# Two merge-gate tiles projected inside the attention stage of a hybrid mixer kernel

## The chip, the cores and the metric

The kernel runs on one core of one Trainium2 chip. The metric is the device time of one execution in microseconds (us). A measurement of it is the median of several executions.

## The reference, cut to what matters

Two layers work on 1024 latent tokens and 256 context tokens of width 1024. In the last layer the context gives keys and values alone, so most projections run over 1280 tokens in layer 0 and over 1024 in layer 1. Everything is float32.

```
z = split_cols(h @ w_in)                     # 54 column tiles of 128 and a short one
y_mla  = dense_attention(...)                # 4 heads, 1280 keys
y_diff = two dense attentions, p1 - lam * p2 # 4 heads, 1280 keys
y_swa  = windowed attention with sinks       # 4 heads, 3 blocks of 128 keys + 256 context keys
y_pool = windowed means, a small matmul
gates  = silu(z.gates)                       # 1024 columns = 8 tiles
mgate  = sigmoid(z.merge)                    # 4096 columns = 32 tiles, 8 for each branch
m = sum_r mgate[r] * ((ys[r] * gates[r]) @ w_br[r])
x = x + gate * rms_norm(m @ w_out)
lam = exp(sum(lam_q1*lam_k1)) - exp(sum(lam_q2*lam_k2)) + lam_init
```

## The kernel before, in words

Activations lie with channels on the partitions. Each float32 matmul is done as three products of rounded halves (`mm3`, L74). A projection tile is 128 columns of `w_in`: for each chunk of tokens (512, 512 and, in layer 0 or for keys and values, 256) it takes 8 steps over the 1024 input channels, and a step is one `mm3`. So a tile is 72 matmuls over 1280 tokens (48 of 512 columns, 24 of 256) and 48 matmuls over 1024 tokens. Its weights come by one transfer of 512 KB (`wraw`), are split into `wh` on ACT and `wl` on POOL, and lie in two buffers; `Dense.step` (L321) asks for the weights of the next tile when it begins one.

A layer has these stages: the latent projections; the other projections, first those that differential attention needs; attention (L1193: units of differential, then MLA, then windowed attention, which is the local branch); the merge (L1400); the output projection.

What is not needed for the first attention units waits in a list of filler tiles (L762 to L772): gates 0 to 6, the tile of windowed values, that of windowed keys, two of windowed queries, two pooling tiles with their small work behind each, gate 7. Attention calls `dense.fill(us)` (L341) after each score block and each step of the probability-times-value products; `fill` adds to an account and issues steps of the list while the account is positive. A step of 512 tokens costs 0.648 in the account's own units, one of 256 half of that; a tile over 1280 tokens costs 12.96, one over 1024 costs 10.37. The amounts stand in `FILL` (L1562): `"pre"` is spent before the first unit; the entries 2, 1 and 3 are the amount for a unit of differential, MLA and windowed attention, shared over its calls (9, 7 and 5 in a full unit; a unit of the context block has fewer). When the list is empty, `fill` does nothing.

Each engine runs its instructions in a fixed order, that of a planner which takes the program's order as priority and moves an instruction forward where it judges it ready first. All transfers are issued by SP's one queue, in such an order too.

In the merge, for each of 32 tiles (branch r, tile d), the gate tile is projected (`st.body`, L1423), its PSUM leaves through a sigmoid on ACT into `sg` (three buffers of 512 tokens, one of 256), and the branch's product of the tile before (`branch_mm`, L1363) is issued after the first 8 steps. DVE multiplies that product with `sg`, POOL adds it to the sum `m`. `st.load` at the head of a tile asks for the weights of the next.

The constants of attention (four rows for lambda, the sinks, the mask) are loaded after the first unit's keys and queries (`const_loads`, L957) and ahead of the "pre" filling.

Of the kernel before, what the change touches and what calls it, by code (L numbers as in the profile page):

```python
# [32 lines left out]
def kernel(ctx: ExitStack, tc: tile.TileContext, A: dict, out: bass.AP):  # L33
# [73 lines left out]
    xmid = dram.tile([KT, 128, SEQ], F, name="xmid")  # L107
    yd = [dram.tile([4, 128, T], F, name=f"yd{r}") for r in range(4)]
    zgd = dram.tile([8, 128, T], F, name="zgd")
    mq = dram.tile([2, 4, 96, T], R, name="mq")  # L110
    mk = dram.tile([2, 4, 64, T], R, name="mk")
    mkr = dram.tile([2, 32, T], R, name="mkr")
# [388 lines left out]
    def layer(l, es_prev):  # L501
# [15 lines left out]
        def lat_tile(i, dt):  # L517
            return (p1 if i > 2 else p1b).tile([128, T], dt, name=f"n{i}", tag=f"n{i}")
# [172 lines left out]
        def gates(j):  # L691
            def ev(ps, c0, n):
                z = f32("zc", n)
                act(z, ps)
                dma(zgd[j, :, c0:c0 + n], z)
            dense.tile(st, W_G + j, qch, ev)

        def pooled():
            LP = 8 + SEQ + 8 + CTX + 8
            H_, L_ = slice(64, 128), slice(0, 64)  # L700
            wph = p2.tile([128, 2, 128], R, name="wph", bufs=1)
            wpl = p2.tile([128, 2, 128], R, name="wpl", bufs=1)
            spc = p2.tile([128, 2], F, name="spc", bufs=1)
            keep = {}

            def pos(c0):
                return c0 + 8 if c0 < SEQ else c0 + 16

            def weights():
                wpr = f32("zc", 256).rearrange("p (a b) -> p a b", a=2)  # L710
                nc.gpsimd.memset(wpr, 0.0)
                for g in range(4):
                    o = 64 * (g % 2)
                    dma(wpr[o:o + 64, g // 2, o:o + 64], A["w_pool"][l, g])
                split(wpr, wph, wpl)
                dma(spc, A["s_pool"][l].rearrange("(j p) -> p j", p=128))

            for j in range(2):
                def ev(ps, c0, n, j=j):
                    if c0 == 0:  # L720
                        vals.drain()
                        if j == 0:
                            weights()
                        keep[j] = p2.tile([128, LP], F, name="up", tag="zt1", bufs=1)
                        nc.gpsimd.memset(keep[j], 0.0)
                    act(keep[j][:, pos(c0):pos(c0) + n], ps)
                dense.tile(st, W_POOL + j, qch, ev)

                def rest(j=j):
                    for c0, n in qch:  # L730
                        up = keep[j][:, pos(c0) - 8:pos(c0) + n + 8]
                        w = n + 16
                        a = f32("t1", w)
                        b = f32("t2", w)
                        tt(a[:, 1:w], up[:, 0:w - 1], up[:, 1:w], ALU.add)
                        if j == 0:
                            tt(b[H_, 8:8 + n], a[H_, 7:7 + n], a[H_, 9:9 + n], ALU.add)
                        else:
                            tt(b[:, 2:w - 1], a[:, 1:w - 2], a[:, 3:w], ALU.add)
                            tt(a[:, 4:w - 3], b[:, 2:w - 5], b[:, 6:w - 1], ALU.add)  # L740
                            tt(b[H_, 8:8 + n], a[H_, 4:4 + n], a[H_, 12:12 + n], ALU.add)
                        yield 0.3 * n / 512
                        nc.vector.tensor_copy(out=b[L_, 8:8 + n], in_=a[L_, 8:8 + n])
                        rc = f32("tab", n)
                        dma(rc, A["rcnt"][j, :, c0:c0 + n])
                        t1 = f32("tab", n)
                        tt(t1, b[:, 8:8 + n], rc, ALU.mult)
                        tt(t1, t1, up[:, 8:8 + n], ALU.subtract)
                        hl_ = {}
                        spl(t1, lambda h: hl_.__setitem__(0, h), lambda h: hl_.__setitem__(1, h))  # L750
                        ps = dense_ps(n)
                        mm3(ps, lambda k: wph[:, j], lambda k: wpl[:, j], lambda k: hl_[0], lambda k: hl_[1], [0], 1)
                        yv = f32("zc", n)
                        act(yv, ps, scale=spc[:, j:j + 1])
                        dma(yd[0][j, :, c0:c0 + n], yv)
                        yield 0.4 * n / 512
                dense.add(f"pool{j}", None, rest)
# [5 lines left out]
        values(W_DV + 1, dvd, 2)  # L763
        roped(W_DK, dkd, ALL, 1.0, 8, 16, ("C32", "S32"))
        roped(W_DQ, dqd.rearrange("m a d n -> a m d n"), qch, 32 ** -0.5, 8, 16, ("C32", "S32"))
        for j in range(7):
            gates(j)
        values(W_SV, svd, 0)
        keys_swa()
        roped(W_SQ, sqd, qch, 64 ** -0.5, 4, 32, ("C64", "S64"))  # L770
        pooled()
        gates(7)  # L772

        p1b = pool(f"mlb{l}", 1, es_m)

# [5 lines left out]
        def wsplit(name, r0, rows, cols):  # L781
# [4 lines left out]
            split(raw, h, lo)  # L786
            return h, lo

        gkv = gcol("g_ckv", 0, 128)
        gq0 = gcol("g_cq", 0, 128)  # L790
        gq1 = gcol("g_cq", 128, 64)
# [97 lines left out]
        def up_all():  # L889
            nonlocal kvh, kvl, q0h, q1h, q0l, q1l  # L890
            for us in key_rope():
                yield us
            kvh, kvl, q0h, q0l = (lat_tile(i, R) for i in (0, 3, 1, 4))
            q1h, q1l = (lat_tile(i, R)[0:64] for i in (2, 5))
            todo = [(0, c) for c in ALL] + [(1, c) for c in qch]
# [51 lines left out]
        c1 = pool(f"ac{l}", 1, es_a)  # L947

        smask = c1.tile([128, 768], F, name="smask")
        ls = c1.tile([128, 2], F, name="ls")  # L950
        nlam = c1.tile([128, 1], F, name="nlam")
        sink = c1.tile([128, 4], F, name="sink")
        nsink = c1.tile([128, 4], F, name="nsink")
        lam = kp.tile([128, T], F, name="P", tag="P", bufs=5)[:, 0:128].rearrange("p (a c) -> p a c", a=4)
        lt = kp.tile([128, T], F, name="P", tag="P", bufs=5)[:, 0:64].rearrange("p (a c) -> p a c", a=2)

        def const_loads():  # L957
            for i, n in enumerate(("lam_q1", "lam_k1", "lam_q2", "lam_k2")):
                dma(lam[:, i], A[n][l:l + 1, :].broadcast_to([128, 32]))
            dma(sink, A["sink"][l:l + 1, :].broadcast_to([128, 4]))  # L960
            dma(smask, A["smask"])

        def const_values():
            lv = lam.rearrange("p (a b) c -> p a b c", b=2)
            tt(lt, lv[:, :, 0], lv[:, :, 1], ALU.mult)
            nc.vector.tensor_reduce(out=ls, in_=lt, axis=AX.X, op=ALU.add)
            act(ls, ls, AF.Exp)
            tt(nlam, ls[:, 1:2], ls[:, 0:1], ALU.subtract)
            ts(nlam, nlam, -lam_init, op0=ALU.add)
            ts(nsink, sink, -1.0)  # L970
# [246 lines left out]

        todo = []
        prefetch(0)
        const_loads()  # L1220
        dense.fill(FILL[l]["pre"])
        const_values()
        last.clear()
        for i, (key, keys, load, run) in enumerate(units):
            mains, after = run(kvs[key], qts.pop(i))
            us, turns = FILL[l][key[0]], TURNS[key[0]]
            f = us / (len(mains) + sum(turns)) if i else 1.6
            for a, main in enumerate(mains):
                main()
                if a == 0:  # L1230
                    prefetch(i + 1)
                dense.fill(f)
                n = turns[a]
                while todo and (todo[0][0] < i - 1 or a and n):
                    todo.pop(0)[1]()
                    dense.fill(f)
                    n -= 1
            todo += [(i, g) for g in after()]
            nxt = units[i + 1][0][0] if i + 1 < len(units) else None
            if nxt != key[0] and key[0] != 2:  # L1240
                close_row(key[0])
# [3 lines left out]
        while pend:  # L1245
            dense.fill(1.0)
            pend.pop(0)()
        dense.until(W_G + 7)
        es_a.close()
        es_p.close()  # L1250

# [147 lines left out]

        for q, (r, d) in enumerate(order):  # L1400
            i = W_M + r * 8 + d
            if q + 1 < len(order):
                st.load((l, i + 1))
            else:
                st.load((l, W_O), use=0)
            braw = tp.tile([128, 2, 128], F, name="braw", tag="braw", bufs=1)
            dma(braw, A["w_br"][l, r, d])
            bh = tp.tile([128, 2, 128], R, name="bh", tag="bh")
# [1 line left out]
            split(braw, bh, bl)  # L1410
            sg = {}

            def ev(ps, c0, n, sg=sg):
                if n == 512:
                    sg[c0] = tp.tile([128, 512], F, name="sg", tag="sg", bufs=3)
                else:
                    sg[c0] = tp.tile([128, 256], F, name="sgc", tag="sgc", bufs=1)
                act(sg[c0], ps, AF.Sigmoid)
            if r < 3 and d == 4:
                prep.add(gated_y(r + 1, 0), 0.0)  # L1420
            if r and d == 0:
                prep.add(gated_y(r, 1), 0.0)
            body = st.body((l, i), qch, ev)  # L1423
            some(body, KT)
            if prev:
                if prev[1] == 0:
# [104 lines left out]
        for q, (ci, d) in enumerate(steps):  # L1531
# [27 lines left out]
        es_l.close()  # L1559
        return es_t  # L1560

    FILL = ({1: 4.1, 2: 4.9, 3: 0.8, "n": 1.5, "uk": 1.2, "uq": 1.5, "uv": 2.0, "pre": 10.0},  # L1562
            {1: 4.3, 2: 4.9, 3: 0.8, "n": 2.5, "uk": 1.2, "uq": 1.5, "uv": 2.0, "pre": 8.0})
    TURNS = {1: (3, 2), 2: (2, 1, 1, 1), 3: (1, 2)}
    GY = (3.0, 1.5, 1.3, 0.5)
    WMB = 6
# [111 lines left out]
```

## Time and profile before

| what | value |
|---|---|
| median of 3 runs | 2753.53 us (2751.33 to 2753.72) |
| profiled execution | 2753.32 us, of it 2751.5 us from the first to the last instruction |
| TensorE's granted clock over the span | 0.978 of full |
| busy: PE, weight load, DVE, ACT, POOL | 95%, 80%, 55%, 43%, 29% |
| layer 0: attention, merge begins | 250 us, about 811 us |
| layer 1: attention, merge begins | 1696 us, about 2197 us |

The page of the profile gives busy time by engine and by slice of the span. The view of instructions by line and shape gives counts and mean durations; the view of stretches gives busy time between two moments; the view in order of time gives single instructions. PE is the matmul engine. A matmul's row is as long as the matmul takes from its start to its last result, and the next begins before that, so PE's busy time overlaps itself and is no measure of how many columns go through.

### The profile page before, as it was taken

To read this page: it belongs to the slowest core of one execution; us is meant where nothing else is said; L and a number is where in the kernel's file an instruction comes from. 1 tells how busy PE (TensorE), PEld (TensorE's weight loads), DVE (VectorE), ACT (ScalarE), POOL (GpSimd) and SP (SyncE) were. 2 spreads that over 40 slices of the span, in tenths; PEclk is the share of its full clock that TensorE was granted. 3 is DMA by queue.
4 is the path that set the end of the run, shared out by engine and by line. 5 is a ranking of instruction groups with operands and counts; after the bars stand their busy time and mean duration, and the time that the engine had idled before them with its cause. 6 is when DMAs were issued, how large, how long until landed. Compare 5 with 4: busy or idle time off the path is not lost.

```text
span 2751.5 us, 38436 instructions
## 1 busy us (share of the span) xinstructions
PE 2616.2 (95%) x14194; PEld 2199.9 (80%) x14194; DVE 1519.6 (55%) x2638; ACT 1186.6 (43%) x2178; POOL 802.3 (29%) x492
## 2 busy tenths in 40 slices
PE   7997999999989989999999997999999999999998
PEld 5776888888878878888878776888877788888878
DVE  7545788766754894332148554888666732233133
ACT  4433677655662212222245443777555722222231
POOL 4223333110002224443324313443110022444324
PEclk9998999999999999999999998999999999999999
DMA  6366333533334652221135266333432243222123
GB/s 237 98 194 202 121 96 92 148 117 96 95 113 141 196 164 77 77 74 61 35 107 193 90 203 210 116 106 113 132 104 91 79 128 103 79 86 87 48 77 100
DMA packets 209069, 322.27 MB, mean 117 GB/s; under 512 B 26740, under 2 KB 123634, under 8 KB 208882
## 3 DMA queue, kind: packets, MB, share of 16 engines
q1 hardware_dynamic: 208882, 319.83, 37.2%
q8 instruction: 111, 1.82, 0.3%
q14 instruction: 76, 0.62, 0.1%
HBM read 239.07 MB, written 77.86 MB: 115 GB/s over the span
## 4 chain that ended last, share of the span: by engine, by line
PE 61%; DVE 9%; issue 4%; DMA 4%; ACT 2%; POOL 1%; SPq 1%; POOLq 0%; DVEq 0%; ACTq 0%
PE pd L76 12%; PE pd L77 12%; PE pd L78 12%; PE acc L1021 5%; PE pt L1005 4%; PE pt L76 2%; PE pt L77 2%; PE pt L78 2%; DVE mjunk L150 2%; PE pss L1116 1%; PE pss L1075 1%; PE pss L1076 1%; PE pss L1077 1%; PE pd L1546 1%; PE pss L1174 1%
## 5 line engine op out<-in xcount | busy, mean ns | idle before, releaser
L76 PE MATMUL pd<-h,wh 128*128 128x512 f32 (+2 forms) x2288 | 857.8, 375 | 20.0 <-ACT zt L50 9.5
L78 PE MATMUL pd<-h,wl 128*128 128x512 f32 (+2 forms) x2288 | 845.4, 370 | 0.0
L77 PE MATMUL pd<-h,wh 128*128 128x512 f32 (+2 forms) x2288 | 844.6, 369 | 0.0
L53 POOL TENSOR_TENSOR wl<-wraw,wh 128x1024 fp32r<-128x1024 f32 x106 | 260.7, 2459 | 988.9 <-ACT wh L50 915.3
L76 PEld LDWEIGHTS pd<-h,wh 128*128 128x128 f32 (+1 forms) x2288 | 436.4, 191 | 83.4 <-ACT sg L50 10.2
L78 PEld LDWEIGHTS pd<-h,wl 128*128 128x128 f32 (+1 forms) x2288 | 435.2, 190 | 67.6 <-issue 1.5
L77 PEld LDWEIGHTS pd<-h,wh 128*128 128x128 f32 (+1 forms) x2288 | 436.6, 191 | 59.0 <-DVE h L56 0.8
L53 DVE TENSOR_TENSOR tl<-pt,th 128x512 fp32r<-128x512 f32 (+1 forms) x420 | 276.3, 671 | 135.0 <-ACT th L50 131.4
L977 DVE CUSTOM_DVE_ANT_0 P<-pss,zero 128x1280 f32<-128x1280 f32 (+1 forms) x216 | 295.9, 1370 | 97.4 <-PE pss L1116 46.1
L50 ACT ACTIVATE th<-pt 128x512 fp32r<-128x512 f32 (+1 forms) x420 | 239.7, 582 | 159.7 <-PE pt L1005 153.1
L53 DVE TENSOR_TENSOR sg<-sg,pt 128x512 f32<-128x512 f32 x96 | 65.6, 687 | 391.0 <-PE pt L78 390.5
L1005 PE MATMUL pt<-kc,P 128*128 128x128 f32 x1632 | 256.2, 276 | 4.8 <-DVE P L56 1.2
L1021 PE MATMUL acc<-th,vt 128*128 128x256 f32 x816 | 244.9, 312 | 3.4 <-ACT ot L50 1.5
L1021 PE MATMUL acc<-tl,vt 128*128 128x256 f32 x816 | 222.0, 293 | 9.5 <-DVE tl L53 8.9
L50 ACT ACTIVATE wh<-wraw 128x1024 fp32r<-128x1024 f32 x124 | 130.8, 1055 | 221.6 <-PE pd L77 169.1
L50 ACT ACTIVATE P<-P,m 128x1280 f32<-128x1280 f32 (+1 forms) x144 | 182.7, 1269 | 75.5 <-DVE m L977 74.7
L50 ACT ACTIVATE sg<-pd 128x512 f32<-128x512 f32 x128 | 75.7, 591 | 311.7 <-PE pd L78 304.4
L1005 PEld LDWEIGHTS pt<-kc,P 128*128 128x128 f32 x1632 | 191.8, 142 | 20.2 <-DVE tl L53 6.3
L53 POOL TENSOR_TENSOR m<-m,sg 128x512 f32<-128x512 f32 x96 | 131.3, 1373 | 209.9 <-DVE sg L53 208.7
L1021 PEld LDWEIGHTS acc<-th,vt 128*128 128x128 f32 x816 | 155.7, 191 | 37.6 <-ACT th L50 20.5
L1021 PEld LDWEIGHTS acc<-tl,vt 128*128 128x128 f32 x816 | 156.1, 191 | 29.5 <-DVE tl L53 20.3
L50 ACT ACTIVATE P<-P,negm 128x1280 f32<-128x1280 f32 (+3 forms) x144 | 146.5, 1017 | 75.2 <-DVE negm L977 74.6
(291 smaller groups left out, 3918.2 us busy)
## 6 DMA issues: line engine op xcount, KB each, us to landing
wraw<-in_w_in_dram SPq DMA_DIRECT2D x108, 512.0 KB, 3.6
wmt<-in_w_modt_dram SPq DMA_DIRECT2D x64, 256.0 KB, 3.0
wraw<-in_w_out_dram SPq DMA_DIRECT2D x32, 512.0 KB, 3.2
yd<-ot SPq DMA_DIRECT2D x108, 128.0 KB, 1.8
kt<-dkd SPq DMA_DIRECT2D x64, 160.0 KB, 3.2
qt<-dqd SPq DMA_DIRECT2D x72, 128.0 KB, 2.8
ya<-yd SPq DMA_DIRECT2D x36, 256.0 KB, 3.0
yb<-yd SPq DMA_DIRECT2D x36, 256.0 KB, 3.0
```

The costliest lines, as they stand in the source:

```text
L50: return nc.scalar.activation(out=o, in_=i, func=func, **kw)
L53: return (e or nc.vector).tensor_tensor(out=o, in0=a, in1=b, op=op)
L76: nc.tensor.matmul(ps, wh(k), xh(k), start=k == 0, stop=False)
L77: nc.tensor.matmul(ps, wh(k), xl(k), start=False, stop=False)
L78: nc.tensor.matmul(ps, wl(k), xh(k), start=False, stop=k == n - 1)
L150: nc.vector.tensor_tensor_reduce(out=jk, in0=a, in1=b, scale=1.0, scalar=start, op0=ALU.mult, op1=ALU.add, accum_out=o)
L977: nc.vector.tensor_tensor_reduce(out=o, in0=i, in1=zero.to_broadcast([128, nk]) if mask is None else mask, scale=-1.0, scalar=1e30 if h is ...
L1005: t = nc.tensor.transpose(pt[:, 2 * j + i, :], Ps[i][:, (g + j) * 128:(g + j + 1) * 128], ident)
L1021: nc.tensor.matmul(acc, vt[:, kts[g + j], :], x[:, j, :], start=g + j == 0 and a == 0, stop=g + j == nk - 1 and a == 1)
L1075: nc.tensor.matmul(o, qt[0:96, 0, qs], kh[0:96, ks], start=True, stop=False)
L1076: nc.tensor.matmul(o, qt[0:96, 0, qs], kl[0:96, ks], start=False, stop=False)
L1077: nc.tensor.matmul(o, qt[0:96, 1, qs], kh[0:96, ks], start=False, stop=True)
```

## The change

Gate 7 joins gates 0 to 6 at the head of the filler list. At its end come two merge-gate tiles, `W_M + 26` and `W_M + 29` (branch 3, tiles 2 and 5). They leave PSUM through a copy on ACT and go to memory (`zmd`). In the merge these two tiles load no weights and issue no projection: each chunk is read back from `zmd` into `sg` and takes its sigmoid there. The loads of the tiles around them skip them. The four lambda rows and the sinks are loaded earlier, before the latent up-projections, and the lambda sums are formed there; the mask is loaded in the third attention unit. `FILL` has new amounts.

```diff
-        for j in range(7):
+        for j in range(8):
             gates(j)
...
         pooled()
-        gates(7)
+        early = [W_M + 26, W_M + 29]
+        for e, i in enumerate(early):
+            merge_gate(e, i)
...
+        def merge_gate(e, i):
+            def ev(ps, c0, n):
+                z = f32("zc", n)
+                act(z, ps)
+                dma(zmd[e, :, c0:c0 + n], z)
+            dense.tile(st, i, qch, ev)
...
+        lam = p1.tile([128, 4, 32], F, name="lam")
+        for i, n in enumerate(("lam_q1", "lam_k1", "lam_q2", "lam_k2")):
+            dma(lam[:, i], A[n][l:l + 1, :].broadcast_to([128, 32]))
+        dma(sink, A["sink"][l:l + 1, :].broadcast_to([128, 4]))
...
         prefetch(0)
-        const_loads()
         dense.fill(FILL[l]["pre"])
...
                 if a == 0:
                     prefetch(i + 1)
+                    if i == 2:
+                        dma(smask, A["smask"])
...
-        dense.until(W_G + 7)
+        dense.until(early[-1])
...
-            if q + 1 < len(order):
-                st.load((l, i + 1))
-            else:
+            if q + 1 == len(order):
                 st.load((l, W_O), use=0)
+            elif i not in early:
+                st.load((l, i + 2 if i + 1 in early else i + 1))
...
+            def reload(e, sg_tile=sg_tile):
+                for c0, n in qch:
+                    s = sg_tile(c0, n)
+                    dma(s, zmd[e, :, c0:c0 + n])
+                    for k in range(KT - 1):
+                        yield 0.0
+                    act(s, s, AF.Sigmoid)
+                    yield 0.0
...
-            body = st.body((l, i), qch, ev)
+            body = reload(early.index(i)) if i in early else st.body((l, i), qch, ev)
...
-    FILL = ({1: 4.1, 2: 4.9, 3: 0.8, "n": 1.5, "uk": 1.2, "uq": 1.5, "uv": 2.0, "pre": 10.0},
-            {1: 4.3, 2: 4.9, 3: 0.8, "n": 2.5, "uk": 1.2, "uq": 1.5, "uv": 2.0, "pre": 8.0})
+    FILL = ({1: 3.95, 2: 6.8, 3: 1.45, "n": 1.5, "uk": 1.2, "uq": 1.5, "uv": 2.0, "pre": 15.0},
+            {1: 3.9, 2: 5.9, 3: 1.45, "n": 2.5, "uk": 1.2, "uq": 1.5, "uv": 2.0, "pre": 13.0})
```

## Rows read from the trace of the kernel before

**Rows 1.** The page's first part: busy us, share of span, instructions.

```profile
PE 2616.2 (95%) x14194; PEld 2199.9 (80%) x14194; DVE 1519.6 (55%) x2638; ACT 1186.6 (43%) x2178; POOL 802.3 (29%) x492
```

**Rows 2.** Stretches: length; PE, PEld, DVE, ACT, POOL busy (instructions); clock; DMA share, GB/s.

```profile
270.00:480.00 210.00, 206.18 (x1266) 174.61 (x1264) 168.25 (x300) 149.00 (x258) 80.55 (x41) 1.00 0.35 107
...
1720.00:1890.00 170.00, 169.56 (x1008) 142.55 (x1007) 144.32 (x233) 126.40 (x203) 73.75 (x33) 1.00 0.34 107
...
2300.00:2400.00 100.00, 100.00 (x439) 82.16 (x438) 27.29 (x38) 23.16 (x37) 36.27 (x22) 1.00 0.29 94
```

**Rows 3.** PE in order of time, full clock: start us, duration us, then the instruction.

```profile
230.18 0.40 PE L76 MATMUL pd<-h,wh 128*128 128x512 f32 x1
...
241.09 0.28 PE L76 MATMUL pd<-h,wh 128*128 128x256 f32 x1
...
243.84 0.28 PE L78 MATMUL pd<-h,wl 128*128 128x256 f32 x1
...
690.02 0.60 PE L1005 MATMUL pt<-kc,P 128*128 128x128 f32 x4
690.38 0.48 PE L76 MATMUL pd<-h,wh 128*128 128x512 f32 x1
```

**Rows 4.** PE by line and shape, 1720 to 1890 us (differential attention, layer 1).

```profile
L76 PE MATMUL pd<-h,wh 128*128 128x512 f32 x103 | 41.5, 403 | 0.0
...
L1021 PE MATMUL acc<-th,vt 128*128 128x256 f32 x130 | 40.0, 318 | 0.1
L1005 PE MATMUL pt<-kc,P 128*128 128x128 f32 x261 | 38.9, 273 | 0.4 <-DVE P L56 0.2
...
L1116 PE MATMUL pss<-kt,qt 128*128 128x512 f32 x104 | 33.6, 404 | 0.0
L1116 PE MATMUL pss<-kt,qt 128*128 128x256 f32 x52 | 14.5, 279 | 0.0
```

**Rows 5.** The same, 270 to 480 us (layer 0): first and last of 11.

```profile
L1005 PE MATMUL pt<-kc,P 128*128 128x128 f32 x298 | 45.3, 273 | 1.2 <-DVE P L56 1.0 <-POOL P L53 0.2
...
L76 PE MATMUL pd<-h,wh 128*128 128x256 f32 x56 | 15.9, 285 | 0.0
```

**Rows 6.** The same, 2125 to 2195 us (windowed attention, layer 1).

```profile
L1005 PE MATMUL pt<-kc,P 128*128 128x128 f32 x164 | 28.6, 278 | 1.9 <-DVE tl L53 0.7 <-ACT P L50 0.4
L1021 PE MATMUL acc<-th,vt 128*128 128x256 f32 x83 | 25.8, 322 | 0.7 <-ACT ot L50 0.6
...
L1174 PE MATMUL pss<-kt,qt 128*128 128x256 f32 x79 | 16.6, 305 | 0.9 <-DMA kt<-skd 0.7
L1174 PE MATMUL pss<-kt,qt 128*128 128x384 f32 x48 | 12.3, 338 | 0.0
```

**Rows 7.** The same, 720 to 765 us (windowed attention, layer 0): first, last of 11.

```profile
L1005 PE MATMUL pt<-kc,P 128*128 128x128 f32 x92 | 15.0, 273 | 0.0
...
L78 PE MATMUL pd<-h,wl 128*128 128x256 f32 x7 | 2.1, 294 | 0.0
```

**Rows 8.** SP's queue in order of time, start of attention, layer 0.

```profile
245.66 0.59 SPq L72 DMA_DIRECT2D P<-in_lam_q_dram  x1
...
250.01 0.43 SPq L72 DMA_DIRECT2D wraw<-in_w_in_dram  x1
```

**Rows 9.** PE there; in brackets the idle time before, and what ended it.

```profile
250.36 1.40 PE L1116 MATMUL pss<-kt,qt 128*128 128x512 f32 x3 [6.24 <-DMA P<-in_lam_k_dram]
...
257.84 0.63 PE L76 MATMUL pd<-h,wh 128*128 128x512 f32 x1
```

**Rows 10.** Tensor `zgd` (the gates): its writes, first and last start; its transfers' time.

```profile
L72 SPq DMA_DIRECT2D zgd<-zc x40: 319/332/607, 250.5 to 2116.8; - x40
...
DMA to landing us min/median/max: 1.7/2.9/6.3
```

**Rows 11.** Tile `sg` of the merge: ns min/median/max, first and last start.

```profile
L50 ACT ACTIVATE sg<-pd x128: 576/597/602, 816.7 to 2640.7; 128x512 f32<-128x512 f32 x128
...
L53 POOL TENSOR_TENSOR m<-m,sg x96: 1262/1300/2213, 985.1 to 2645.5; 128x512 f32<-128x512 f32 x96
```

More of the change, by code (lines that the diff above doesn't have):

```diff
@@ L109 @@
     zgd = dram.tile([8, 128, T], F, name="zgd")
+    zmd = dram.tile([2, 128, T], F, name="zmd")
     mq = dram.tile([2, 4, 96, T], R, name="mq")
@@ L787, in wsplit @@
             return h, lo
+        ls, nlam, sink, nsink = (sta.tile([128, w], F, name=n) for n, w in (("ls", 2), ("nlam", 1), ("sink", 4), ("nsink", 4)))
+        lam = p1.tile([128, 4, 32], F, name="lam")
+        for i, n in enumerate(("lam_q1", "lam_k1", "lam_q2", "lam_k2")):
+            dma(lam[:, i], A[n][l:l + 1, :].broadcast_to([128, 32]))
+        dma(sink, A["sink"][l:l + 1, :].broadcast_to([128, 4]))
         gkv = gcol("g_ckv", 0, 128)
@@ L892, in up_all @@
                 yield us
+            lv = lam.rearrange("p (a b) c -> p a b c", b=2)
+            tt(lv[:, :, 0], lv[:, :, 0], lv[:, :, 1], ALU.mult)
+            nc.vector.tensor_reduce(out=ls, in_=lv[:, :, 0], axis=AX.X, op=ALU.add)
             kvh, kvl, q0h, q0l = (lat_tile(i, R) for i in (0, 3, 1, 4))
@@ L949, in layer @@
         smask = c1.tile([128, 768], F, name="smask")
[L950 to L961, printed above, removed]
         def const_values():
-            lv = lam.rearrange("p (a b) c -> p a b c", b=2)
-            tt(lt, lv[:, :, 0], lv[:, :, 1], ALU.mult)
-            nc.vector.tensor_reduce(out=ls, in_=lt, axis=AX.X, op=ALU.add)
             act(ls, ls, AF.Exp)
@@ L1411, in layer, with sg_tile @@
             sg = {}
-            def ev(ps, c0, n, sg=sg):
+            def sg_tile(c0, n, sg=sg):
                 if n == 512:
@@ L1417, in ev @@
                     sg[c0] = tp.tile([128, 256], F, name="sgc", tag="sgc", bufs=1)
-                act(sg[c0], ps, AF.Sigmoid)
+                return sg[c0]
+            def ev(ps, c0, n, sg_tile=sg_tile):
+                act(sg_tile(c0, n), ps, AF.Sigmoid)
+            def reload(e, sg_tile=sg_tile):
[6 more added lines that the diff above has]
+                    yield 0.0
             if r < 3 and d == 4:
```

## The prediction

> **What bounds the kernel now.** I read the page's busy shares first: PE 95%, no other engine above 55% [rows 1]. Then the stretches: PE is busy 100 of 100 us in the merge of layer 1, 169.6 of 170 in its differential attention, 206.2 of 210 in that of layer 0 [rows 2]. Such a row hides short waits, so I went to single instructions. From the first 512-column matmul of a run of 48 to the next shape are 10.91 us, so one comes each 0.227 us; 24 of 256 columns follow at 0.12 us; four 128-column transposes take 0.36 us, 0.09 each [rows 3]. Each shape's count by its spacing gives the time PE needs. In layer 1's differential stretch: 307 projection matmuls of 512 columns (three rows like the first) 69.8 us, 24 of 256 (three rows of 8) 2.9, 260 value products (two rows of 130) 31.2, 261 transposes 23.5, scores 23.6 and 6.2: 157 of 170 us [rows 4]. So 13 us, 8%, are short waits for DVE and ACT. The same sum over the 11 rows of layer 0's stretch gives 190 of 210 [rows 5]. In the merge 439 matmuls in 100 us are their spacing and nothing more [rows 2, 3]: there PE's issue is the bound. In the windowed attention of layer 1, which has no filler, 164 x 0.09, 166 x 0.12 (two rows of 83), 79 x 0.12 and 48 x 0.17 (384 columns, an estimate between its neighbours) make 52 of 70 us [rows 6]: 18 us, 25%, unused.
>
> **The change part by part.** The number of matmuls stays. Two tiles leave the merge, 2 x (48 x 0.227 + 24 x 0.12) = 27.6 us in layer 0 and 2 x 48 x 0.227 = 21.8 in layer 1, and the same matmuls come back in attention. So the gain is what they find there of unused PE time, and their place decides.
>
> *Where the filler lands.* Counting the `fill` calls of the loop in order, with both sets of amounts, gives the position in the filler list, in the account's units: after "pre", after differential, after MLA, at the end. Layer 0 before: 10.4, 102.1, 173.9, 184.9; after: 15.6, 140.3, 209.6, 210.9. Layer 1 before: 8.4, 86.8, 153.1 (empty in the last MLA unit); after: 13.6, 106.6, 168.7, 173.9. The last write of a gate at 2116.8 us, where layer 1's MLA ends, bears the count out [rows 10]. One unit is 1.06 us of PE (13.8 us for 12.96). So, in us of PE:
> layer 0: pre +5.5, differential +35.0, MLA -2.7, windowed -10.3, merge -27.6;
> layer 1: pre +5.5, differential +15.4, MLA -4.5, windowed +5.5, merge -21.8.
> Each sums to nothing. The local branch itself gets less than its 1.45 a unit says, for the list is empty when it begins (layer 0) or two units later (layer 1); the work goes into differential attention.
>
> *How much an attention stage absorbs.* No row shows differential attention with more filler, so I bound it: at best all its unused time, 21 us in layer 0 and 14 in layer 1 (20 and 13 carried to the whole stage), at worst none. The nearest rows are windowed attention with and without filler. With: 45 us hold 67 score matmuls, 8 to a unit, so 5.4 us a unit, with 36 x 0.227 + 23 x 0.12 = 10.9 us of filler, 1.3 a unit [rows 7]. Without: 127 scores in 70 us, 4.4 a unit [rows 6]. So 1.3 us cost 1.0, and 23% is absorbed. I take 23%: 8.1 us in layer 0's differential stage, 3.5 in layer 1's, 1.3 in layer 1's windowed; layer 0's windowed stage loses 10.3 us of filler and so 2.4 of cover. MLA takes its change at full price.
>
> *The rule against it.* Weight loads fill 142.6 of 170 us in the differential stretch, 84%, and 82.2 of 100 in the merge [rows 2]. The Trainium skill (Perfetto Trace Analysis, Identifying the Most-Contended Engine) holds matmul busy time to be a poor measure of TensorE's headroom, and the share of weight-load time a good one. The first half agrees with the 100% and 99.7% of the two stretches. By the second half the differential stage has no more room than the merge, and the sum would be that of the first rival below. By the spacing it has 8%; a transpose has a weight load of its own for only 128 columns, so I go by the spacing.
>
> *Start of attention.* PE idles 6.2 us before the first score, and the first product of the second gate tile comes at 257.84 us, with the first scores between [rows 9]. Its weights are asked for at 250.01, behind lambda, sinks and mask, which hold SP's queue from 245.66 [rows 8]: 4.35 us that go. The 5.5 us of "pre" then start up to 4.35 us sooner, in time that PE spends waiting. Half of that, 2.5 us (rounded up), in each layer; bounds 0 and 4.35, and below nothing by the second rival.
>
> *What I cost at nothing.* The constants' five issues move into the projections, at 0.43 to 0.59 us each as in [rows 8], with two DVE instructions; PE's projections cover them; without cover 2 to 3 us a layer. The two tiles' weight transfers and splits move with them, same in number. Ten copies out of PSUM come to attention's ACT, 0.6 us each [rows 11], 6 us in all; ACT is busy 126 of 170 us there [rows 2]; at worst 6. Ten writes and ten reads of at most 256 KB are new. The new wait is the read-back: it waits in SP's queue for a slot of `sg`, and behind it stand the branch weights and the next tile's weights, due a tile (13.6 us) later. In layer 1 the second chunk's slot is free once the product before is added: 6 x 0.227, a DVE product taken as long as POOL's sum, and that sum, 1.3, make 4.0 us after that branch product began [rows 3, 11]; transfer 2.9 and sigmoid 0.6 make 7.5 [rows 10, 11]. It is wanted behind 12 + 24 + 12 matmuls, at 10.9 us. Three us are to spare; the longest transfer seen, 6.3, takes them all [rows 10].
>
> *The sum.* Absorbed: 8.1 + 3.5 + 1.3 - 2.4 = 10.5 us; starts 5.0; together -15.5. From the profiled execution's 2753.3 (span 2751.5 and 1.8 around it; 0.2 below the median) that is 2737.8, and so 2738.
>
> **The rivals.** *A wash.* Differential attention absorbs nothing and the starts give nothing: -15.5 + 11.6 + 5.0 = +1.1, 2754 us. For it: DVE is busy 144 and ACT 126 of 170 us there, near PE's 157, so the short waits may not be free to fill [rows 2, 4]. Against it: more independent matmuls between a score and the products that need it.
>
> *Slower: the first score queued behind "pre".* The fixed order could put the second gate tile's first chunk, now part of "pre" and so earlier in the program, ahead of the first score. PE would wait for its weights, until 257.84 - 4.35 = 253.5 us, and do 24 matmuls at half clock (three scores take 1.40 us there [rows 9]), 24 x 0.454 = 10.9: the first score comes at 264.4 and not 250.4, 14 us late, of which 5.5 are work done. 8.5 us a layer, in place of a gain of 2.5: -15.5 + 22 = +6.5, 2760 us. It decides if the first score starts after that tile's first product. Against it: now the order puts scores ahead whose data come sooner.
>
> *The merge does not give back.* The read-back is late by 3 us a tile, through a transfer of 9 us: +12, 2750 us. Against it: the three us to spare.
>
> *More.* All unused time of both differential stages is filled: 35 for 11.6, 2714 us. For it: more distance between dependents is what short waits lack.
>
> **How the numbers follow.** Forecast, with absorption of 10 to 45% in differential attention: 0.55. Wash: 0.17. Slower: 0.10. Merge: 0.06. More: 0.12. Low end: half of the unused time absorbed and full starts, -15.5 - 6 - 4 = -25, is 2728; I go to 2722, toward the fourth rival, and up to 2756, past the wash. Fewer than 2 in 10 are left out, most of it above. A change of 0.2%, 5.5 us, is about what a measurement of this kernel can tell from none. Faster by more: the forecast (0.54 of it), the fourth rival, and a little of the third: 0.68. Within: the wash and most of the third: 0.21. Slower: the second and the wash's upper tail: 0.11.
>
> **What would show it.** In the changed kernel's trace: gate 7 written before the windowed values' tile, in differential attention; `zmd` written at the end of MLA; windowed attention nearly without projection matmuls in both layers, at 4.4 us a unit; the merge shorter by 27 and 22 us with PE still at 100%; differential attention with its start longer by 30 and 15 us, its PE need above 92% of the stretch; the first score at about 250 us with the second gate tile's products near 254. I am wrong if differential attention grows by all its filler, if a score waits behind that tile, or if the merge shows idle PE at its tiles 26 and 29.

## The result, and the profile after

The changed kernel takes 2793.12 us (median; 2787.10 to 2795.32) against 2753.62 (2751.33 to 2755.56) beside it: 1.0141 times as long [1.0129, 1.0153], 39.5 us slower. The forecast was 2738 us, 15.5 us faster, with a range to 2756. The profiled execution took 2795.32 us, its span is 2793.5.

The page's busy shares, which answer to [rows 1], barely move:

```profile
PE 2622.4 (94%) x14194; PEld 2213.0 (79%) x14194; DVE 1531.6 (55%) x2638; ACT 1191.9 (43%) x2188; POOL 799.4 (29%) x492
```

The matmul count is the same and PE is busy 6 us longer, in a span 42 us longer. So most of the loss is time in which PE does nothing. I cut the span at the first score of each attention branch and at the first and last product of a branch in the merge (order-in-time view):

| stage, us | layer 0 before, after | change | forecast | layer 1 before, after | change | forecast |
|---|---|---|---|---|---|---|
| differential | 241.5, 293.7 | +52.2 | +29.9 | 212.0, 245.5 | +33.5 | +14.9 |
| MLA | 217.8, 225.4 | +7.6 | -2.7 | 210.9, 211.2 | +0.3 | -4.5 |
| windowed | 120.7, 110.1 | -10.6 | -7.9 | 95.2, 96.9 | +1.7 | +4.2 |
| merge | 552.4, 528.1 | -24.3 | -27.6 | 426.9, 405.7 | -21.2 | -21.8 |

The forecast column is the prediction's own terms (differential with "pre", the start's gain and the absorbed part). The merge gave back nearly all it should. Differential attention is 41 us worse than forecast, MLA 15.

The view of stretches shows it directly. Columns as in [rows 2]; the first two rows run from 20 us after a layer's first score to the first score of MLA, the third is in the merge. After:

```profile
271.00:544.70 273.70, 247.91 (x1489) 214.57 (x1488) 192.72 (x349) 169.06 (x300) 93.79 (x50) 0.98 0.35 106
1743.80:1969.30 225.50, 204.61 (x1197) 173.96 (x1195) 166.63 (x276) 146.48 (x242) 86.76 (x40) 0.98 0.33 104
2300.00:2400.00 100.00, 100.00 (x448) 82.31 (x447) 26.09 (x41) 23.59 (x38) 30.16 (x14) 1.00 0.32 102
```

The same two stretches before:

```profile
270.40:491.90 221.50, 217.42 (x1335) 183.74 (x1333) 177.14 (x322) 157.58 (x275) 86.07 (x45) 1.00 0.34 105
1716.60:1908.60 192.00, 190.71 (x1134) 159.77 (x1132) 162.57 (x268) 142.06 (x230) 82.33 (x37) 1.00 0.36 111
```

Length less PE busy is 25.8 and 20.9 us after, 4.1 and 1.3 before. I call the sum of the two **the idle time**: it goes from 5.4 to 46.7 us. That is 41.3 more, in the stage that is 41 us worse than forecast.

A part of the loss is clock. The granted clock of these two stretches is 1.00 before and 0.98 after: for 20 us of them it stood at the lower of its two levels, 1.2 GHz. It did so in five pieces, each of which begins inside an idle time of PE of 1.8 to 3.6 us or up to 1.5 us behind it. The longest (clock 0.50):

```profile
283.30:290.10 6.80, 5.56 (x16) 4.60 (x17) 5.48 (x8) 3.51 (x5) 0.00 (x0) 0.50 0.29 96
```

In another, a matmul of 512 columns took 0.43 us to the next (321.17 to 321.60), where [rows 3] have 0.227. So 20 us at this level cost about 10 us, an estimate.

What ended it, from the view of waits (engine, tile and line, what it waited for; us, times, longest), first DVE's over layer 0's differential stage, then PE's. After:

```profile
DVE P L980 <- PE pss L1119: 37.5, 31, 13.0
DVE P L980 <- POOL P L53: 29.2, 11, 4.5
...
PE pss L1119 <- DVE m L980: 19.2, 9, 3.6
```

Before:

```profile
DVE P L977 <- PE pss L1116: 26.9, 25, 3.9
...
DVE P L977 <- POOL P L53: 4.1, 5, 1.2
...
PE pss L1116 <- DVE m L977: 4.2, 3, 1.8
```

The changed kernel's lines are 3 to 5 further down here: DVE's softmax step (L980, L977 before) writes a probability tile `P`. It now waits for POOL's mix, which scales one such tile and adds it to a second, and PE's next score waits for DVE to have read the one score buffer. One unit, in order of time (start us, duration us; in brackets the idle time and what ended it), after:

```profile
453.78 1.49 DVE L980 CUSTOM_DVE_ANT_0 P<-pss,zero 128x1280 f32<-128x1280 f32 x1 [0.25 <-PE pss L1119]
...
455.33 0.85 PE L1119 MATMUL pss<-kt,qt 128*128 128x512 f32 x3
455.58 1.33 POOL L64 TENSOR_SCALAR P<-P,s 128x1280 f32<-128x1280 f32 x1 [10.53 <-DVE s L56]
...
457.00 2.93 POOL L53 TENSOR_TENSOR P<-P 128x1280 f32<-128x1280 f32 x1
...
459.96 1.49 DVE L980 CUSTOM_DVE_ANT_0 P<-pss,zero 128x1280 f32<-128x1280 f32 x1 [2.80 <-POOL P L53]
...
461.52 0.39 PE L1119 MATMUL pss<-kt,qt 128*128 128x256 f32 x1 [1.95 <-DVE m L980]
...
463.75 0.60 PE L1008 MATMUL pt<-kc,P 128*128 128x128 f32 x4
```

A unit of before:

```profile
396.79 1.35 POOL L64 TENSOR_SCALAR P<-P,s 128x1280 f32<-128x1280 f32 x1 [6.38 <-PE pt L1005]
...
398.05 0.60 PE L1005 MATMUL pt<-kc,P 128*128 128x128 f32 x4
398.22 2.96 POOL L53 TENSOR_TENSOR P<-P 128x1280 f32<-128x1280 f32 x1
398.58 1.49 DVE L977 CUSTOM_DVE_ANT_0 P<-pss,zero 128x1280 f32<-128x1280 f32 x1 [0.58 <-PE pt L1005]
...
400.48 0.74 PE L1116 MATMUL pss<-kt,qt 128*128 128x512 f32 x3
```

The mix is as long in both (1.3 + 2.9 us). Before, DVE's softmax runs beside it, into a free tile. After, the softmax starts as the mix ends (457.00 + 2.93 = 459.93), 3.78 us after its three score matmuls were done on PE at 456.18. There are five `P` tiles, used again and again: a ring. A unit makes four and frees two by the mixes; the other two are held until their last transposes on PE. Those of the unit ahead, the `pt` rows above, end at about 398.6 before, 1.0 us after this unit's fourth scores, and release the fourth softmax. After, they end at 464.35, 8.2 us after the fourth scores. In all full units behind a full unit, of both layers, it is 0.8 to 1.8 us before and 1.4 to 10.8 after. Of 30 fourth softmaxes (full units but the first of each layer) these transposes released 21 before and none after; the mix released 2 before and 23 after. The program puts filler between the steps that hold these transposes.

The rest of the trace. Start of attention, PE (answers to [rows 9]):

```profile
251.05 1.41 PE L1119 MATMUL pss<-kt,qt 128*128 128x512 f32 x3 [7.70 <-DMA qt<-dqd]
253.11 0.79 PE L76 MATMUL pd<-h,wh 128*128 128x512 f32 x1 [0.66 <-ACT wh L50]
```

The two reloaded tiles: writes of `zmd`, its reads of 512 tokens, the sigmoids' wait for these, and their transfers' time (view of `sg`):

```profile
L72 SPq DMA_DIRECT2D zmd<-zc x10: 319/323/543, 712.8 to 2201.3; - x10
L72 SPq DMA_DIRECT2D sg<-zmd x8: 326/326/383, 1323.6 to 2655.1; - x8
...
  ACT sg L50: 7.7, 4
...
DMA to landing us min/median/max: 2.6/3.1/3.5
```

### The profile page after: what moved, and what is told of

It is laid out like the page before. It is cut to its first block, busy times and chain, and to the rows that moved or that the text cites. A ratio compares the mean times of both kernels' runs of the same rounds, so it can differ in the third digit from the quotient of the medians.

```text
span 2793.5 us, 38486 instructions
## 1 busy us (share of the span) xinstructions
PE 2622.4 (94%) x14194; PEld 2213.0 (79%) x14194; DVE 1531.6 (55%) x2638; ACT 1191.9 (43%) x2188; POOL 799.4 (29%) x492
## 5 line engine op out<-in xcount | busy, mean ns | idle before, releaser
L76 PE MATMUL pd<-h,wh 128*128 128x512 f32 (+2 forms) x2288 | 869.0, 380 | 23.6 <-ACT sg L50 11.1
L980 DVE CUSTOM_DVE_ANT_0 P<-pss,zero 128x1280 f32<-128x1280 f32 (+1 forms) x216 | 295.4, 1368 | 165.6 <-PE pss L1119 67.4
L1008 PE MATMUL pt<-kc,P 128*128 128x128 f32 x1632 | 262.0, 277 | 6.0 <-DVE P L56 1.7
L1024 PE MATMUL acc<-th,vt 128*128 128x256 f32 x816 | 231.7, 299 | 3.5 <-ACT ot L50 2.5
L1024 PE MATMUL acc<-tl,vt 128*128 128x256 f32 x816 | 223.0, 293 | 12.7 <-DVE tl L53 11.6
L1008 PEld LDWEIGHTS pt<-kc,P 128*128 128x128 f32 x1632 | 193.3, 142 | 19.1 <-DVE tl L53 6.4
L1024 PEld LDWEIGHTS acc<-tl,vt 128*128 128x128 f32 x816 | 156.7, 192 | 33.5 <-DVE tl L53 22.3
```

The lines of the kernel that those rows point to most:

```text
L76: nc.tensor.matmul(ps, wh(k), xh(k), start=k == 0, stop=False)
L980: nc.vector.tensor_tensor_reduce(out=o, in0=i, in1=zero.to_broadcast([128, nk]) if mask is None else mask, scale=-1.0, scalar=1e30 if h is ...
L1008: t = nc.tensor.transpose(pt[:, 2 * j + i, :], Ps[i][:, (g + j) * 128:(g + j + 1) * 128], ident)
L1024: nc.tensor.matmul(acc, vt[:, kts[g + j], :], x[:, j, :], start=g + j == 0 and a == 0, stop=g + j == nk - 1 and a == 1)
```

## The experiments

The ring theory (Theory A in the texts below): the larger amounts make PE reach the last transposes of a unit later, all five `P` tiles are taken, and the softmax waits for POOL's mix. Rivals: the new list or the constants are to blame; the mix on POOL is dear whatever the filler; POOL's queue is late through the filler's weight splits; or the filler simply costs its full time. Each edit also lets the planner write another order, so no run changes one wait alone. "Idle" is the idle time defined above, from each run's own two rows. "Before" stands at 2753.6 us beside the change and at 2755.4 to 2757.2 beside the others, so a difference to the change, taken below from the times as they stand, would be 2 to 4 us larger (smaller where the run is slower) if each were taken from the before beside it.

| run | us | ratio to before | idle |
|---|---|---|---|
| before | 2753.6 | 1 | 5.4 |
| the change | 2793.1 | 1.0141 [1.0129, 1.0153] | 46.7 |
| new_list_old_amounts | 2732.9 | 0.9915 [0.9899, 0.9932] | 5.9 |
| old_list_new_amounts | 2802.2 | 1.0160 [1.0145, 1.0175] | 46.6 |
| diff_amount_4_9 | 2731.8 | 0.9909 [0.9894, 0.9923] | 10.9 |
| diff_amount_middle | 2752.3 | 0.9987 [0.9977, 0.9997] | 24.0 |
| steps_earlier | 2754.7 | 0.9989 [0.9977, 1.0000] | 12.7 |
| mix_on_dve | 2732.1 | 0.9913 [0.9899, 0.9928] | 0.8 |
| before_constants_early | 2748.5 | 0.9972 [0.9962, 0.9982] | 5.3 |
| before_steps_earlier | 2751.4 | 0.9984 [0.9975, 0.9994] | 4.7 |
| before_mix_on_dve | 2746.2 | 0.9968 [0.9956, 0.9981] | 1.3 |
| mix_on_dve_amount_4_9 | 2713.8 | 0.9852 [0.9839, 0.9866] | 2.2 |
| amount_4_9_steps_earlier | 2728.4 | 0.9905 [0.9890, 0.9921] | 6.8 |
| mix_dve_4_9_steps_earlier | 2741.6 | 0.9949 [0.9932, 0.9966] | 8.4 |
| two_key_tiles | 2798.1 | 1.0143 [1.0127, 1.0158] | 33.5 |
| six_tiles | 2784.6 | 1.0093 [1.0074, 1.0112] | 19.1 |
| splits_on_dve | 2789.0 | 1.0108 [1.0087, 1.0129] | 39.8 |
| six_tiles_splits_on_dve | 2777.4 | 1.0072 [1.0051, 1.0094] | 14.4 |

**Which part of the change?** The changed kernel with the old `FILL`, and the kernel before with the new one.

```diff
-    FILL = ({1: 3.95, 2: 6.8, 3: 1.45, ..., "pre": 15.0},
-            {1: 3.9, 2: 5.9, 3: 1.45, ..., "pre": 13.0})
+    FILL = ({1: 4.1, 2: 4.9, 3: 0.8, ..., "pre": 10.0},
+            {1: 4.3, 2: 4.9, 3: 0.8, ..., "pre": 8.0})
```

> The changed kernel with the amounts of before. Theory A (the larger amounts stretch differential attention: the last transposes of a unit come later, its probability tiles stay taken, DVE's fourth softmax waits for POOL's mix, and PE for DVE): differential attention falls back from 294 and 245 us to about 242 and 212, and the whole to 2745 to 2760 us, with some 23 and 6 us of the list left for behind attention. Theory B (the earlier constants, the order of the list or the read-back cost it): within 6 us of 2793.

> The kernel before with the new amounts alone; nothing else is changed. Theory A: differential attention 285 to 295 and 240 to 246 us, MLA shorter by some 28 and 20 us since its filler runs out, the whole 2770 to 2785. Theory B: differential attention longer by no more than its filler, 41 and 21 us, and the whole at 2754 or less.

The amounts lose and the list wins: the list with the old amounts is 24 us faster than before, the new amounts without the list are 45 us slower, with the same idle time as the change. Both lie outside the ranges I gave for Theory A, on the side that makes its effect larger: below 2745 and above 2785.

**Which amount?** Only differential attention's entry goes back, all the way or about half.

```diff
-    FILL = ({1: 3.95, 2: 6.8, ...},
-            {1: 3.9, 2: 5.9, ...})
+    FILL = ({1: 3.95, 2: 4.9, ...},
+            {1: 3.9, 2: 4.9, ...})
```

> The changed kernel with one number undone: differential attention's amount is 4.9 in both layers; the rest of the new amounts stays, so the two merge tiles fall into windowed attention. Theory A: differential attention about 247 and 217 us (5 us of pre more than before), windowed attention takes 26 and 20 units of filler and absorbs a quarter, the whole 2738 to 2752. Theory B: within 8 us of 2793.

> The changed kernel with 5.8 and 5.4 for differential attention's 6.8 and 5.9, between them and 4.9. If each unit of filler costs alike there: halfway between 2732 and 2793, 2758 to 2768. Theory A with a threshold (the tiles run out once the last transposes come behind the fourth score): one layer or both still without the wait, 2735 to 2752.

With 4.9 the run is 61 us below the change, and 6 below the range I gave; with 5.8 and 5.4 it lies 41 below it and 20 above 4.9. That is under the straight line between the two (2761) and at the edge of what a threshold would give: the loss grows faster than the amount. Idle time follows, 10.9, 24.0, 46.7.

**Do earlier value steps free the tiles?** The products of a unit take five steps, each with its transposes, that the program places behind the score blocks of later units. By the places 2, 1, 1, 1 three of them stand behind the second to fourth block of the next unit and two behind the first block of the unit after it. By 0, 2, 3, 0 all five stand ahead of the next unit's fourth block. All the filler is left in.

```diff
-    TURNS = {1: (3, 2), 2: (2, 1, 1, 1), 3: (1, 2)}
+    TURNS = {1: (3, 2), 2: (0, 2, 3, 0), 3: (1, 2)}
```

> The changed kernel with all five value steps of a unit of differential attention issued within the next unit and ahead of its fourth score block (turns 0, 2, 3, 0 for 2, 1, 1, 1); amounts and all else as changed. So the two probability tiles of the unit before are free when the fourth softmax wants one. Theory A: DVE's wait for POOL's mix goes from 29 and 28 us to under 8, differential attention to 265 to 280 and 220 to 235 us, the whole to 2745 to 2775. Theory C (PE's fixed order puts scores too early whatever tiles are free): DVE's wait for POOL may go, but differential attention stays within 8 us of 294 and 245.

> The kernel before with the value steps of differential attention issued earlier (turns 0, 2, 3, 0). Theory A: DVE waits only 5 us for POOL's mix there, so freeing the tiles sooner gains little: within 8 us of before. Rival: the earlier steps are a gain of their own, whatever the amounts, and the 38 us they gave the changed kernel come here too: near 2720.

38 us come back in the changed kernel, 5 in the one before, and DVE's wait for the mix in layer 0's stage is 3.7 us where it was 29.2. The stretches of steps_earlier:

```profile
267.00:525.40 258.40, 247.80 (x1517) 213.57 (x1515) 196.49 (x347) 168.86 (x300) 94.91 (x50) 0.99 0.37 111
1721.30:1925.70 204.40, 202.34 (x1208) 172.42 (x1207) 167.18 (x280) 147.59 (x243) 86.25 (x39) 1.00 0.38 116
```

**Is it POOL's mix?** The first row tile's mix as one DVE instruction, as the second's already is; and the same edit in the kernel before.

```diff
-                            if i == 0:
-                                ts(P2, P2, r, 1.0, ALU.mult, ALU.mult, nc.gpsimd)
-                                tt(P, P, P2, ALU.add, nc.gpsimd)
-                            else:
-                                stt(P, P2, r, P, ALU.mult, ALU.add)
+                            stt(P, P2, r, P, ALU.mult, ALU.add)
```

> The changed kernel with the mix of the two probability maps of the first query half on DVE (one instruction of 1.55 us, as for the second half) and not on POOL (1.33 and 2.95 us). Theory A: DVE's wait for POOL is gone and PE's unused time falls by at least half of the 20 and 18 us that came, though DVE has 25 us more to do in each stage; differential attention 270 to 288 and 225 to 240, the whole 2755 to 2782. Theory C (PE's order): 2785 or more.

> The kernel before, with the first row tile's mix of the two probability tiles as one instruction on DVE in place of two on POOL. Ring theory (the extra filler makes the probability tiles come free later, and POOL's mix is then what holds them): with the old filler DVE waited for POOL's mix only 4.1 us in layer 0's differential stage and 1.0 in layer 1's, so there is little to win: 2748 to 2758 us against 2756. Rival (the mix on POOL is dear by itself, whatever the filler): the 61 us that the same edit took off the changed kernel come back here in good part, 2700 to 2740 us.

61 us come back, more than expected, and 9 in the kernel before, which is a little more than the ring theory allowed and far from the rival's. With all the filler in, mix_on_dve has PE idle for 0.8 us:

```profile
267.60:511.10 243.50, 243.37 (x1521) 213.72 (x1519) 208.73 (x366) 170.32 (x302) 28.89 (x12) 1.00 0.39 117
1706.90:1908.40 201.50, 200.80 (x1203) 173.04 (x1202) 185.96 (x295) 147.59 (x243) 24.51 (x10) 1.00 0.39 117
```

**Do the cures add?** Old differential amounts with each of them, and all three.

> The changed kernel with both: the mix on DVE, and the differential amounts back at 4.9. Ring theory: with 4.9 the wait was nearly gone already (PE waited 1.7 us for DVE's maximum in layer 0's stage), so the two edits don't add: 2724 to 2734 us, beside 2732 for either alone. If what each removes is a cost of its own, they add: about 2732 - 24 = 2708 us or less.

> The changed kernel with the differential amounts at 4.9 and the value steps at the earlier places (0, 2, 3, 0) within a unit. Ring theory: the earlier places took 38 us where the ring was late, and 5 where it was not (the kernel before); with 4.9 it is hardly late, so 2725 to 2732 us. If the places are worth by themselves what they gave with the large amounts: 2694 us.

> The changed kernel with three edits: mix on DVE, amounts 4.9, value steps at (0, 2, 3, 0). Ring theory: with the mix off POOL no tile is held late, so the earlier steps have nothing left to win: 2709 to 2716 us beside the 2713.8 without them. If the earlier steps have a worth of their own (5 us in the kernel before, 3 with 4.9): 2706 to 2710.

The first was not as I expected: 2713.8 us is 18 below either alone, outside the overlap (2724 to 2734) and 6 above the sum. The mix's move is worth 9 us in the kernel before and 18 in the changed kernel, both with 4.9 for differential attention, and 61 with 6.8 and 5.9: the mix on POOL costs something even where the ring is hardly late, and much more where it is. This is the best version of the study, 0.9852 of before. The second came as expected. The third missed both expectations, 28 us slower than without the steps. From the first score of differential attention to that of windowed attention the two layers are 26 us longer together (885.8 for 859.6). PE's idle time over the whole of these stages is 16 us of that (36.3 for 20.6), 9 of them in MLA; the rest is in waits too short to be idle rows. The trace shows one thing that the new order does: in 26 of 30 units DVE does two subtractions of the value products between its mix and the fourth softmax (without the steps one, in 5 of 30), and that softmax starts 2.3 us after its scores (median) where it started 1.0. That this makes the 26 us is not shown.

**Is it the number of tiles?** A sixth `P` tile had room only with two key tiles in place of three, so that is the control.

```diff
-            return kp.tile([128, T], F, name="P", tag="P", bufs=5)[:, 0:nk]
+            return kp.tile([128, T], F, name="P", tag="P", bufs=6)[:, 0:nk]
...
-            return kp.tile([128, T], R, name="kt", tag="kt", bufs=3)
+            return kp.tile([128, T], R, name="kt", tag="kt", bufs=2)
```

> The changed kernel with two key tiles in place of three: the control of the run beside it, which needs their room. Both theories: the next head's first key tile can no longer be loaded ahead, so at most some 20 changes of head cost up to a transfer of 3 us each: 2793 to 2850 us.

> The changed kernel with six probability tiles in place of five, and two key tiles in place of three for the room. Ring theory (too few tiles for the places of the transposes): DVE's wait for POOL's mix goes from 57 us to under 10, and the run is 35 to 50 us below the one with two key tiles beside it. Rival (it is POOL's mix as such, its 4.3 us between the last softmax of a row tile and its transposes or its hold on a shared resource, and not the number of tiles): within 10 us of that control.

The sixth tile gives 13.5 us, against 35 to 50 expected. DVE's wait for the mix over the whole run does fall, from 57.5 us in the changed kernel and 23.3 in the control to 7.3, and idle time by 14.4. The stretches of the control:

```profile
266.30:545.50 279.20, 260.02 (x1541) 221.16 (x1540) 191.61 (x349) 171.16 (x303) 97.68 (x51) 0.98 0.35 102
1736.30:1971.00 234.70, 220.40 (x1253) 184.69 (x1252) 174.10 (x283) 150.04 (x248) 92.16 (x42) 0.97 0.35 102
```

Those with six tiles:

```profile
272.90:537.80 264.90, 255.33 (x1546) 217.39 (x1544) 194.10 (x353) 172.16 (x305) 98.53 (x51) 0.99 0.36 106
1735.20:1956.20 221.00, 211.48 (x1225) 177.50 (x1225) 171.48 (x277) 149.23 (x244) 88.52 (x40) 0.99 0.34 101
```

The control is a poor one: against the before beside it, it is no faster than the change (1.0143 and 1.0141) though its idle time is 13.2 less, so some 13 to 18 us go elsewhere, and six_tiles carries these too. With six tiles the fourth softmaxes hardly wait: from the end of their scores to their start pass 8.8 us in the 30 units together (98.3 in the changed kernel, 59.4 in the control, 31.2 before). Yet the run is 28 us slower than before. So the ring is a cause, but for 14 us only is it shown alone.

**Is POOL late through the splits?** One of the longest gaps after has a weight split of the filler inside the mix, on POOL's queue:

```profile
312.08 1.34 POOL L64 TENSOR_SCALAR P<-P,s 128x1280 f32<-128x1280 f32 x1 [11.83 <-DVE s L56]
313.38 2.41 POOL L53 TENSOR_TENSOR wl<-wraw,wh 128x1024 fp32r<-128x1024 f32 x1
315.74 2.90 POOL L53 TENSOR_TENSOR P<-P 128x1280 f32<-128x1280 f32 x1
318.67 1.49 DVE L980 CUSTOM_DVE_ANT_0 P<-pss,zero 128x1280 f32<-128x1280 f32 x1 [4.52 <-POOL P L53]
320.22 0.39 PE L1119 MATMUL pss<-kt,qt 128*128 128x256 f32 x1 [3.50 <-DVE m L980]
```

```diff
-            self.add(i, lambda: st.load((self.l, i)), lambda: ...)
+            self.add(i, lambda: st.load((self.l, i), e=None), lambda: ...)   # split on DVE
```

> The changed kernel with the weight splits of the filler's tiles on DVE in place of POOL; the mix stays on POOL, five probability tiles. Queue theory (a sixth tile gave only 13 us because POOL's mix is itself late: in layer 0 two of the three longest gaps of TensorE, 3.75 and 3.68 us, have a weight split of 2.4 us ahead of the mix or inside it on POOL): half or more of the 40 us come back, 2750 to 2772 us. Ring alone: the 4.3 us of the mix are enough to be late, and only the few gaps with a split shorten: 2780 to 2793. Splits on DVE dear by themselves (DVE stands between two scores): above 2793.

> Both: six probability tiles (two key tiles for the room) and the filler's weight splits on DVE. Queue theory: DVE's wait for POOL's mix goes under 3 us, and the time under both of the runs it combines, 2745 to 2765 us (six_tiles alone 2784.6). If neither the ring nor the queue holds the rest: 2775 to 2790.

The splits are worth 4 us alone (7 from the before beside each), as the ring alone would have it, and 7 beside the sixth tile. Idle time falls by 6.9 and 4.7. As the main cause this rival falls. But the second run lies in the range that I gave for the rest being neither the ring nor the queue: 21 us of loss against before remain.

**Are the constants worth what I gave them?** The kernel before with the lambda rows and sinks loaded early and the mask in the third unit, as in the change.

> The kernel before with the constants' loads and the lambda sums moved as in the change, the mask in the third unit; list, amounts and merge as before. If the 4.35 us of SP's queue ahead of the second gate tile's weights were what held up the start: first products of that tile 4 to 9 us sooner in both layers, first score 1 to 4 us sooner, the whole 2740 to 2751 beside 2757 of before on the chip of the runs above. If the transfers of keys and queries alone set the start: within 4 us of before.

Faster by 8 us, [0.9962, 0.9982]; I had put 5.0 on the two starts.

**What follows.** The amounts of differential attention make the loss, through the wait for POOL's mix: the smaller amounts, the mix elsewhere and the earlier steps each remove most of the idle time and 38 to 61 us with it. That the mix holds up PE is shown: moved, it gives 61 us with the large amounts and 9 in the kernel before. How its cost divides between the tiles' number and the order that the planner makes around it stays open: the sixth tile explains a third at most, with a poor control, and the run with three edits is explained by neither.

## Why the prediction was wrong

*What bounds the kernel now.* The count held: by the same spacings differential attention needs PE for 210 us of 241.5 in layer 0 and 188 of 212.0 in layer 1. The unused 31 and 24 us are more than the 21 and 14 that the prediction bounds the stage with, because the stage's first 20 us, at a granted clock of 0.65 and 0.71, hold some 10 and 8 of them. That the rest is "short waits for DVE and ACT" was right; what I did not ask is which of them grow when filler is put in.

*Where the filler lands.* Right in the main. PE's need by the spacings rises in differential attention by 32 us in layer 0 and 15 in layer 1, where the count gave 40.5 and 20.9 with "pre". The missing 9 and 6 turn up in MLA, as filler that PE does after MLA's first score: in layer 0, 240 projection matmuls of 512 columns follow it where 202 did.

*How much an attention stage absorbs.* This is the step that failed. I bounded it between all of the unused time and "at worst none", and took 23%, 8.1 and 3.5 us. The unused time (length less need at full clock) grew, from 31 to 52 us and from 24 to 42. Instead of -11.6 the term measured +38, a miss of 50 in a total of 55; about 10 of the 38 are the lower clock. The bound of nothing had no reason behind it: it supposes that filler only fills, but in a fixed order filler also delays what stands behind it, here the transposes that give the `P` tiles back. The row that I carried over, windowed attention [rows 6, 7], has no mix on POOL. In that stage itself it was about right in layer 0 (10.6 us shorter for 13 less need) and too low in layer 1 (1.7 longer for 5 more). And the room was there: with the mix on DVE and all the filler in, the unused time is 19 and 16 us, 21 less than before the change, and the time 2732.1 us, below the forecast (9 us of that the edit gives without the change).

*The rule against it.* The Trainium skill (Perfetto Trace Analysis, Identifying the Most-Contended Engine) would have had the stage absorb nothing, 2754 us. That was nearer than my 23%, but not for its reason: the stage lost time, and weight loads filled 83% of layer 0's stretch before (183.74 of 221.5), 78% after, and 88% with the mix on DVE (213.72 of 243.5), so 83% was no ceiling. The Trainium skill fits better in another section of Perfetto Trace Analysis, Optimization Strategy, which says that the same gap returning on the engine that should be saturated can mean too few buffers for the next tile. The trace agrees with the gap (PE waited for DVE's maximum 9 times in layer 0's stage, 19.2 us), and the sixth tile agrees with the cause for 14 us of the time.

*Start of attention.* The second gate tile came at 253.11 us, as foreseen near 254, and the first score did not queue behind it. But the first score was held by its queries until 251.05, so the stage did not begin sooner in this profile. What gain there is lies behind that score: the 20 us from it hold 70 matmuls where they held 52, and 73 in layer 1 where they held 62. The constants alone gave 8 us for the two layers.

*What I cost at nothing.* Right where it was tested by the trace: the merge is 24.3 and 21.2 us shorter, the reads of 512 tokens from `zmd` land in 3.1 us (3.5 at most; the prediction used 2.9), ACT waits 7.7 us for them, and PE's wait for `sg` is 11.1 us where it was 9.4. POOL's mix is not in that list, because I looked only at what the change adds.

*The rivals.* "Slower" named a score behind "pre", which did not happen; 2793 lay beyond the forecast and all four rivals. The result came from a mechanism that no rival had: an old instruction, not moved, whose cover was moved away. The forecast of the sign would have been right for the list alone: 24 us faster with the old amounts.

## What to carry to other kernels

Unused time of an engine that runs in a fixed order is not room by itself: filler put between the producer and the last reader of a tile lengthens that tile's life, so count the tiles of the ring that are alive and ask which engine hands the next one back, and how long its step is. Look at the waits that are short or absent now and stand one filler step from the path. When a chain crosses a slow engine, moving that one step (here 4.3 us on POOL to 1.55 on DVE) can be worth more than rearranging the filler, and parts are tried one by one, since here the list and the constants were good and one amount lost more than they gave.

## What the runs showed of the hardware

A DVE instruction with two inputs on one column per partition, 0.22 us in most places, lasted until POOL's two-input instruction beside it had ended. In the changed kernel, in order of time:

```profile
488.91 2.40 POOL L53 TENSOR_TENSOR wl<-wraw,wh 128x1024 fp32r<-128x1024 f32 x1
489.11 2.22 DVE L56 SCALAR_TENSOR_TENSOR s<-s,nlam,ssum 128x1 f32<-128x1 f32 x1
491.37 1.55 DVE L56 SCALAR_TENSOR_TENSOR P<-P,s 128x1280 f32<-128x1280 f32 x1
```

It ends at 491.33, POOL's at 491.31. The Trainium skill (SBUF — State Buffer, Terms) says that the two engines share one pair of ports under a lock held for a whole instruction, with the loser blocked; this row agrees. Of 72 such instructions in the changed kernel three took over 0.5 us, and seven of 72 in the kernel before; each overlapped such a POOL instruction and ended about 0.02 us after it. So it is no cause of the loss. It can hold a mix on DVE too: in mix_dve_4_9_steps_earlier three of 64 took 2.7 to 3.7 us and not 1.55, each beside a weight split on POOL. A softmax step beside POOL keeps its 1.49 us (398.58 in the unit of before above, inside the mix's 398.22 to 401.18).
